# A weight sum of the down-projection taken from the in-projection's fourth block into its second, and the down-projection's buffers in two pools

## The chip, the cores and the metric

One Trainium2 chip, of which one core is used. The metric is the device time of one execution in microseconds (us). Everything is fp32; matmul operands are split into a high and a low fp32r part and multiplied as three matmuls.

## The reference, cut to what matters

One layer of a streaming encoder over 2048 prompt tokens and 8 x 16 sample tokens, width 1024:

```
z   = x @ w_in                      # 1024 -> 2824: mLSTM q, k, v, o, gates; attention q, k, v
mix = [mLSTM heads | sliding-window attention] @ w_out
h   = layer_norm(alpha * x + mix)
u   = h @ w_up                      # 1024 -> 5632, then a causal convolution of width 3
f   = (silu(gate) * value) @ w_down # 2816 -> 1024
y   = layer_norm(alpha * h + f)     # and the states of mLSTM, attention and convolution
```

## The kernel before, in words

The three large products are done with seven block products in the place of eight (a scheme of Strassen's kind), so they need sums and differences of quarters of the weights and of the tokens. The steps of one group carry the numbers 1 to 7 (variable `s`).

**In-projection** (`i_dense`). 17 tiles of 128 tokens stand in four blocks, b = 0 to 3, which the text calls first to fourth. A block has five groups of output columns (g = 0 to 4) and a group has seven products of 24 matmuls (`i_product`, L713). The weights are loaded into `wraw`, split by ScalarE (L218, high part) and VectorE (L219, low part) into a ring of eight halves `w`, four products' worth, and a half comes free when PE has done its product. Between the products, PE does the steps of three chains (mLSTM, attention, sample tokens) for tokens of the block before; ppt (L1354) is a transpose in the attention, pht (L1188) one in the mLSTM, pnum (L1223) its numerator. The chain of the mLSTM's norm runs DVE (statistics L1162, mr L1171), POOL (ms L1172), ACT (hn L1178), PE (pht).

A block's tokens are loaded into four buffers `xr1` to `xr4` (`x_load`, L541), each there once, in the last group of the block before by program order, and turned into operands until the block's own direct products (L739) are done.

**Weight sums** (`d_sums`). The down-projection needs 11 pairs of summed weight rows, kept in DRAM as `zt`. One sum loads two rows of 512 KB (`txy`, L854 and L855), makes four VectorE subtractions in place (L860 to L863) and stores both (L865, L866). While the in-projection runs, its two tiles are taken from the buffers `xr1` and `xr3`; its three parts stand behind the products 6, 5 and 3 of a group. Four of the 11 sums are done there, seven in the out-projection. A counter gives out the row pairs, so that the n-th sum takes pair n wherever it stands.

**Order of the work.** PE's instructions are issued in program order (`manual_schedule`). Those of the other engines and of SP, which issues nearly all DMAs, are put in order by the framework's scheduler, by readiness and program order; each engine and SP then work through their queues in that order. Two tiles with the same tag and bufs=1 take turns in program order.

**Up- and down-projection** (`f_ups`, `f_downs`). The up-projection has two pools on one stack: `f2sb` (operands hh/hl of the products 2, 5 and 3, the halves u0 and u1, ua, ub) and above it `f3sb` (cc, th, the operands of product 4, the convolution's states). Its last steps are the convolution (L1939, L1941), the gate (L1966 to L1968) and the store of cc (L1969, L1971). Both pools are closed then, and `dsb` is opened in their place, with r2, r3, r4 (loaded token operands, L2013, 16.9 KB a partition each; r1 is elsewhere) and six tiles yacc of 4 KB (L2151). The down-projection works through seven products a block (DORDER 1, 2, 4, 6, 5, 3, 7) in six units each; `d_tokens` splits a unit of r into fu, `d_weights` loads and splits weights into uw, and L2099 copies the banks of product 1 before product 2 adds to them.

Of the kernel before, what the change touches and what calls it, by code (L numbers as in the profile page):

```python
# [8 lines left out]
F32 = mybir.dt.float32  # L9
# [5 lines left out]
P = 128  # L15
D = 1024
# [189 lines left out]
class Prog:  # L206
# [20 lines left out]
    def run(self):  # L227
        PS = bass.MemoryType.PSUM
        nb = len(OBLOCKS)
        with ExitStack() as es:  # L230
            def enter(*a, **k):
                cm = self.pool(*a, **k)
                return cm.__enter__(), cm
            close = lambda cm: cm.__exit__(None, None, None)
            self.cp = es.enter_context(self.pool("const"))
            self.dp = es.enter_context(self.pool("dram", space=bass.MemoryType.DRAM))
            es.enter_context(self.tc.manual_schedule(engines={mybir.EngineType.PE}))
            self.setup()
            self.wp = es.enter_context(self.pool("wsb"))
            self.dps = es.enter_context(self.pool("dps", 3, PS))  # L240
            self.tp, tcm = enter("tsb", side="right")
            self.tps, tpcm = enter("tps", 5, PS)
            self.xp, xcm = enter("xsb")
            self.mp, mcm = enter("isb")
            chains = Chains(self)
            self.xs, self.gates, self.i_done = {}, {}, 0
            self.i_begin()
            self.warm_up()
            chains.weave(self.i_dense())
            close(mcm)  # L250
            wx, wxcm = enter("wx1sb")
            self.unit_more(wx)
            self.mp, mcm = enter("osb")
            self.o_setup()
            for b in range(nb - 1):
                chains.weave(self.late_done(self.o_block(b)))
            chains.until(NPT - 1)
            chains.drain()
            close(tpcm)
            close(tcm)  # L260
            self.fp, fcm = enter("fsb", side="right")
            self.fup, fpcm = enter("fup", 3, PS)
            self.f_setup()
            dense = self.o_block(nb - 1)
            first = self.f_hT(0)
            next(first)
            n = 0
            for i, _ in enumerate(dense):
                if i >= 2:
                    next(first, None)  # L270

                if i in (4, 7, 10):
                    self.f_tokens(0, *{4: (1,), 7: ("t1",), 10: ("t3", 7, "t2", 6)}[i])

                if i >= 22 and n < (2, 4, 5)[min((i - 22) // 4, 2)]:
                    self.f_next()
                    n += 1
            for _ in first:
                pass
            assert not self.norms  # L280
            close(mcm)
            close(wxcm)
            close(xcm)

            self.wx, wxcm = enter("wx2sb")
            self.f2, f2cm = enter("f2sb")
            self.f3, f3cm = enter("f3sb")
            self.f_ups(n)
            close(f3cm)
            close(f2cm)  # L290
            self.f2, f2cm = enter("dsb")
            self.f_downs()
            for cm in (f2cm, wxcm, fpcm, fcm):
                close(cm)


# [294 lines left out]
    def i_dense(self):  # L591
        nc, a = self.nc, self.a
        nb = len(IBLOCKS)
# [34 lines left out]
        for item in self.items:  # L628
            if after:

                after[0] -= 1
                if after[0] == 3:
                    self.logs_of(after[1] - 1)
                if after[0] < 0:
                    self.i_done = after[1]
                    after = None
            self.chains.hold = item[0] == "t" and item[1] > 0
            if item[0] == "t":
                _, b, ti, e = item
                if ("g", e, 3) not in self.wu:  # L640
                    self.advance()
                if b not in self.gates:
                    self.gates[b] = self.tp.tile([P, 5, 8], F32, name="gates", tag="gates", bufs=2)
                if b == 0 and ti == 1:
                    for h in range(2):
                        for i in range(2):
                            yield from self.i_direct(b, i, e, self.ib[i * 2], (h,))
                    self.i_keys(b, 0, self.ib[0])
                    self.i_keys(b, 1, self.ib[2])
                    self.advance()  # L650
                    continue
                ps = self.bank([P, 512], "pg") if ti == 4 else self.ib[ti % 2 * 2]
                yield from self.i_direct(b, ti, e, ps)
                self.i_keys(b, ti, ps)
                if ti == 3 and b or ti == 4:
                    self.release(4)
                    self.x_steps(b, 4)
                    if b:
                        self.x_steps(b, 5)
                self.advance()  # L660
                continue
            _, b, g, s = item
            if item not in self.wu:
                self.advance()
            yield from self.i_product(b, g, s)
            del self.wu[item]
            self.release(2)
            if self.trans and s != 4:
                self.i_transposes()
            with self.tc.high_priority():  # L670
                behind = self.i_after(b, g, s)
            if (b, g, s) == (0, 0, 7):
                self.t_setup()
            if (g, s) == (last, 4):
                after = [8, b + 1]
            if g == last and b + 1 < nb:
                if s == 7:
                    for i in (0, 2):
                        self.rope_load(IBLOCKS[b + 1][i], 2)
                for x in passages[b > 0].get(s, ()):  # L680
                    if x == "load":
                        self.spare = True
                        self.x_load(b + 1, 1, 2, 3, 4)
                    else:
                        self.x_steps(b + 1, x)
            if g == last and b + 1 == nb and s in (7, 5, 2, 3):
                self.x_pair(0, (7, 5, 2, 3).index(s))
            with self.tc.issue_after(behind) if behind and b == 0 else nullcontext():
                self.advance()

            if (b, g) in ((nb - 2, 1), (nb - 1, 0), (nb - 1, 1), (nb - 1, 2)):

                steps = (6, 5, 3)
                if s in steps:
                    self.d_sums(sums, steps.index(s))
                    sums += s == steps[2]
# [1305 lines left out]
    def d_load(self, b, q, u):  # L2002

        h, one = self.d_shape(b)
        if u == 0:
            pool, tag = (self.fp, "hraw") if q == 1 else (self.f2, f"r{q}")
            self.dr[b, q] = pool.tile([P, NK2, 384], F32, name=f"r{q}", tag=tag, bufs=1)
        r = self.dr[b, q]
        k0 = 0 if q in (1, 3) else NK2
        c0 = 0 if q in (1, 2) else h  # L2010
        ks = slice(DUNITS[u][0], DUNITS[u][-1] + 1)
        z = self.zf[b][k0:k0 + NK2][ks].rearrange("k p m -> p k m")
        self.nc.sync.dma_start(r[:, ks, :h], z[:, :, c0:c0 + h])  # L2013
        if one and q in (1, 2):
            self.nc.sync.dma_start(r[:, ks, h:h + one], z[:, :, 2 * h:])
# [46 lines left out]
            self.d_load(*l)  # L2062

    def f_downs(self):
        nc, a, f2 = self.nc, self.a, self.f2
        V, S = nc.vector, nc.scalar
        mm = nc.tensor.matmul
        ln2 = []
# [9 lines left out]
        nb, nu = len(FBLOCKS), len(DUNITS)  # L2078
        ys, ops = {}, {}
# [63 lines left out]
        for g, (b, s, u) in enumerate(self.dseq):  # L2143
# [3 lines left out]
            ts = [*tiles[:np_], *tiles[2 * np_:]] if s == 1 else tiles[np_:2 * np_] if s == 2 else []  # L2147
            if 0 <= u - 2 < len(ts):
                t = ts[u - 2]
                ys[t] = f2.tile([P, D], F32, name="yacc", tag="yacc", bufs=6)  # L2150
                nc.sync.dma_start(ys[t], self.zh[t])  # L2151
            if g == 3 * nu:
                for n in ("ln2_g", "ln2_b"):
                    t = self.fp.tile([P, D], F32, name="f_" + n, tag="hst", bufs=2)
# [53 lines left out]
```

## Time and profile before

| | before |
|---|---|
| median of 3 runs | 2300.78 us (2300.11 to 2303.31) |
| the profiled execution | 2301.44 us |
| its span, first to last instruction | 2299.7 us |
| TensorE busy | 2275.3 us (99%) |
| VectorE busy | 1810.8 us (79%) |
| ScalarE busy | 1272.3 us (55%) |
| GpSimd busy | 277.5 us (12%) |
| mean granted TensorE clock | 0.998 |
| DMA | 631.30 MB, 275 GB/s |

The span is the time between the first and the last instruction; the execution's own time is 1.7 us longer. PE is the matmuls on TensorE, PEld its weight loads, DVE is VectorE, ACT ScalarE, POOL GpSimd, SP SyncE. L713 is line 713 of the kernel. out<-in are the tiles that an instruction writes and reads. In the list of waits a row reads: who waited, for whom, us in total, times, the longest one. In the chain of waits a row is: start, us, what. In the timeline: start, us, instruction, and in brackets how long the engine stood idle before it and what ended that.

### The profile page before, as it was taken

How to read it: one execution, taken by the hardware profiler on the slowest of the kernel's cores; microseconds unless marked ns; L12 is line 12 of the kernel's file. 1: busy time of each engine (PE TensorE's matmuls, PEld its weight loads, DVE VectorE, ACT ScalarE, POOL GpSimd, SP SyncE). 2: the span in 40 equal slices, each digit the busy share in tenths (PEclk: the TensorE clock that was granted, in tenths of full speed). 3: DMA queues.
4: the chain of work that ended last, by engine and by line, in shares of the span. 5: the costliest groups of instructions: out<-in, count | busy, mean ns of one | idle time of the engine just before them, and what ended most of it. 6: DMA issues, size and time to landing. Idle time of an engine off the chain costs nothing.

```text
span 2299.7 us, 39828 instructions
## 1 busy us (share of the span) xinstructions
PE 2275.3 (99%) x14293; PEld 2090.5 (91%) x14293; DVE 1810.8 (79%) x3068; ACT 1272.3 (55%) x2373; POOL 277.5 (12%) x509
## 2 busy tenths in 40 slices
PE   8999999999999999999999999999999999999998
PEld 8999999989878778999999999999999978888876
DVE  8787677777688888998778777678766786895987
ACT  5453476766776656555656555556555544444442
POOL 0001001010121210211112000003211200200100
PEclk9999999999999999999999999999999999999999
DMA  7988998899998867898777999988998786757742
GB/s 283 318 304 289 302 327 276 276 309 305 324 324 266 279 212 279 300 331 300 280 273 269 305 300 310 311 267 288 320 295 262 248 298 212 251 173 222 256 153 86
DMA packets 302901, 631.30 MB, mean 275 GB/s; under 512 B 48172, under 2 KB 141424, under 8 KB 302704
## 3 DMA queue, kind: packets, MB, share of 16 engines
q1 hardware_dynamic: 298032, 615.06, 79.1%
q0 software_dynamic: 3520, 10.56, 1.5%
q10 hardware_dynamic: 1152, 3.15, 0.4%
q8 instruction: 113, 1.85, 0.3%
q14 instruction: 84, 0.69, 0.1%
HBM read 457.02 MB, written 171.64 MB: 273 GB/s over the span
## 4 chain that ended last, share of the span: by engine, by line
PE 84%; DVE 2%; DMA 2%; issue 0%; ACT 0%; POOL 0%; SPq 0%; DVEq 0%; POOLq 0%; ACTq 0%
PE dps L1883 20%; PE fup L1883 20%; PE dps L713 9%; PE dps L2091 7%; PE fup L2091 6%; PE fht L2091 6%; PE dps L223 3%; PE dps L225 2%; PE dps L224 2%; PE ppo L1360 1%; PE psc L1315 1%; PE ppt L1354 1%; PE dps L739 1%; PE fht L1707 1%; PE pscore L1140 1%; PE pnum L1223 1%
## 5 line engine op out<-in xcount | busy, mean ns | idle before, releaser
L1883 PE MATMUL fup<-hh,uw 128*128 128x384 f32 (+1 forms) x1848 | 478.2, 328 | 0.0
L1883 PE MATMUL dps<-hh,uw 128*128 128x384 f32 (+1 forms) x1848 | 478.0, 328 | 0.0
L1883 PEld LDWEIGHTS fup<-hh,uw 128*128 128x128 f32 x1848 | 330.3, 188 | 0.0
L1883 PEld LDWEIGHTS dps<-hh,uw 128*128 128x128 f32 x1848 | 330.1, 188 | 0.0
L1883 PE MATMUL fup<-hl,uw 128*128 128x384 f32 (+1 forms) x924 | 302.9, 328 | 0.9 <-DVE hl L219 0.9
L1883 PE MATMUL dps<-hl,uw 128*128 128x384 f32 (+1 forms) x924 | 302.8, 328 | 0.0
L1941 DVE SCALAR_TENSOR_TENSOR cc<-u,cw,cc 128x768 f32<-128x768 f32 (+1 forms) x264 | 258.1, 978 | 38.8 <-ACT cc L1939 30.5
L713 PE MATMUL dps<-w,oh 128*128 128x256 f32 x1344 | 254.7, 285 | 0.0
L218 ACT CAST uw<-wraw 128x1024 fp32r<-128x1024 f32 x126 | 123.2, 978 | 230.1 <-PE dps L2091 122.2
L219 DVE TENSOR_TENSOR w<-wraw,w 128x1024 fp32r<-128x1024 f32 (+2 forms) x163 | 186.3, 1150 | 65.7 <-ACT w L218 63.3
L218 ACT CAST w<-wraw 128x1024 fp32r<-128x1024 f32 (+2 forms) x163 | 160.2, 991 | 114.1 <-PE dps L713 53.6
L713 PEld LDWEIGHTS dps<-w,oh 128*128 128x128 f32 x1344 | 210.8, 188 | 11.0 <-issue 8.1
L219 DVE TENSOR_TENSOR uw<-wraw,uw 128x1024 fp32r<-128x1024 f32 x126 | 142.4, 1131 | 62.1 <-ACT uw L218 61.9
L713 PE MATMUL dps<-w,ol 128*128 128x256 f32 x672 | 188.2, 280 | 0.0
L1883 PEld LDWEIGHTS fup<-hl,uw 128*128 128x128 f32 x924 | 173.6, 188 | 1.7 <-DVE hl L219 1.6
L2091 PE MATMUL fup<-uw,fu 128*128 128x512 f32 x726 | 173.9, 396 | 1.3 <-ACT fht L2099 1.3
L1883 PEld LDWEIGHTS dps<-hl,uw 128*128 128x128 f32 x924 | 173.8, 188 | 0.0
L713 PE MATMUL dps<-oh,w 128*128 128x256 f32 x896 | 167.6, 283 | 2.9 <-DVE w L219 2.2
L2091 PEld LDWEIGHTS fup<-uw,fu 128*128 128x128 f32 x726 | 136.5, 188 | 34.3 <-ACT fht L2099 1.8
L2091 PE MATMUL dps<-uw,fu 128*128 128x512 f32 x660 | 164.9, 396 | 0.0
L2091 PEld LDWEIGHTS dps<-uw,fu 128*128 128x128 f32 x660 | 124.2, 188 | 29.7
L713 PEld LDWEIGHTS dps<-oh,w 128*128 128x128 f32 x896 | 140.0, 188 | 9.6 <-issue 4.9
(320 smaller groups left out, 4569.0 us busy)
## 6 DMA issues: line engine op xcount, KB each, us to landing
uw<-zw SPq DMA_DIRECT2D x176, 512.0 KB, 4.8
zw<-uw SPq DMA_DIRECT2D x88, 512.0 KB, 3.5
w<-zws SPq DMA_DIRECT2D x72, 512.0 KB, 6.0
wv<-wup SPq DMA_DIRECT2D x66, 512.0 KB, 5.0
wraw<-wi SPq DMA_DIRECT2D x65, 512.0 KB, 5.2
wraw<-zt SPq DMA_DIRECT2D x60, 512.0 KB, 3.8
wraw<-wdn SPq DMA_DIRECT2D x45, 512.0 KB, 4.5
wraw<-wo SPq DMA_DIRECT2D x40, 512.0 KB, 4.7
```

The lines of the kernel that those rows point to most:

```text
L218: nc.scalar.copy(hi, src)
L219: return nc.vector.tensor_sub(lo, src, hi.bitcast(F32)).ins
L223: mm(out, ah, bh, start=start, stop=False)
L224: mm(out, ah, bl, start=False, stop=False)
L225: mm(out, al, bh, start=False, stop=stop)
L713: mm(o, l, r, start=s in (1, 7) and c == k == i == 0, stop=k == 3 and i == 2, skip_group_check=True)
L739: mm(o, x, w, start=k == i == 0, stop=k == KD - 1 and i == 2, skip_group_check=True)
L1140: self.nc.tensor.matmul(ps[:, h], qk[:, 4 + h], qk[:, h], start=True, stop=True)
L1223: nc.tensor.matmul(ps[:, i], sd[:, h], v1[:, h], start=True, stop=t == 0)
L1883: mm(ps, l[:, k], r[:, k], start=s in (1, 7) and k == 0 and i == 0, stop=k == 3 and i == 2, skip_group_check=True)
L1941: V.scalar_tensor_tensor(c[:, v], u[:, i:i + n], w[i], c[:, v], op0=ALU.mult, op1=ALU.add)
L2091: mm(ps, l[:, k, c], r[:, k], start=s in (1, 4, 7) and u == 0 and k == 0 and i == 0, stop=u == nu - 1 and k == n - 1 and i == 2, skip_grou ...
```

## The change

In `i_dense` the four places of the in-projection's sums were (block, group) = (2, 1), (3, 0), (3, 1), (3, 2) with b counted from 0; they are now (1, 1), (2, 1), (3, 0), (3, 2). In `run` the pool `dsb` gives way to two, `d2sb` and `d3sb`, opened one above the other; r2 and r3 are in the first, r4 and yacc in the second.

```diff
@@ run
             close(f3cm)
             close(f2cm)
-            self.f2, f2cm = enter("dsb")
+            self.f2, f2cm = enter("d2sb")
+            self.f3, f3cm = enter("d3sb")
             self.f_downs()
-            for cm in (f2cm, wxcm, fpcm, fcm):
+            for cm in (f3cm, f2cm, wxcm, fpcm, fcm):
                 close(cm)
@@ i_dense
-            if (b, g) in ((nb - 2, 1), (nb - 1, 0), (nb - 1, 1), (nb - 1, 2)):
+            if (b, g) in ((1, 1), (nb - 2, 1), (nb - 1, 0), (nb - 1, 2)):
 
                 steps = (6, 5, 3)
                 if s in steps:
                     self.d_sums(sums, steps.index(s))
@@ d_load
-            pool, tag = (self.fp, "hraw") if q == 1 else (self.f2, f"r{q}")
+            pool, tag = (self.fp, "hraw") if q == 1 else (self.f3 if q == 4 else self.f2, f"r{q}")
             self.dr[b, q] = pool.tile([P, NK2, 384], F32, name=f"r{q}", tag=tag, bufs=1)
@@ f_downs
-        nc, a, f2 = self.nc, self.a, self.f2
+        nc, a = self.nc, self.a
...
-                ys[t] = f2.tile([P, D], F32, name="yacc", tag="yacc", bufs=6)
+                ys[t] = self.f3.tile([P, D], F32, name="yacc", tag="yacc", bufs=6)
```

## The prediction

> **What bounds the kernel now.** I read the page first, then the stretches of 50 us, the list of what TensorE waited for, and the chain of waits around the two places that the diff touches.
>
> ```profile
> span 2299.7 us, 39828 instructions
> PE 2275.3 (99%) x14293; PEld 2090.5 (91%) x14293; DVE 1810.8 (79%) x3068; ACT 1272.3 (55%) x2373; POOL 277.5 (12%) x509
> 500.00:550.00 50.00, 46.50 (x378) 42.06 (x379) 31.54 (x104) 31.55 (x81) 5.43 (x9) 0.97 0.94 320
> 1850.00:1900.00 50.00, 48.69 (x209) 39.01 (x208) 47.48 (x55) 24.90 (x32) 0.00 (x0) 1.00 0.78 287
> PE ppt L1354 <- ACT pth L1355: 2.7, 1, 2.7
> PE pht L1188 <- ACT hn L1178: 1.3, 3, 0.5
> PE pnum L1223 <- issue: 1.0, 1, 1.0
> PE ppt L1354 <- DVE C L1235: 0.8, 1, 0.8
> PE fup L2091 <- ACT fht L2099: 1.3, 1, 1.3
> ```
>
> In the stretches the columns after the length are the busy times of PE, PEld, DVE, ACT and POOL, then the granted clock, the DMA share and GB/s. TensorE is busy 2275.3 of 2299.7 us and its instructions are not touched, nor is their order, which is written out by hand. So the change can move only idle PE time, and 24.4 us is all there is. The two windows hold 3.5 and 1.3 us of it. The waits name it: 2.7 + 0.8 us in front of two attention transposes in the fourth in-projection block (b=3), 1.3 us at the start of the down-projection. The 1.0 and the 1.3 us (pnum, pht) belong to the third block (b=2).
>
> The idle time near 512 us has a sequel. These are stretches of 2 us, with PE alone, clock, DMA share, GB/s:
>
> ```profile
> 512.00:514.00 2.00, 0.00 (x0) 1.00 1.05 385
> 514.00:516.00 2.00, 1.82 (x6) 0.57 0.92 291
> 516.00:518.00 2.00, 2.00 (x9) 0.57 0.55 217
> 518.00:520.00 2.00, 2.00 (x19) 1.00 0.77 242
> ```
>
> Behind the 2.7 us without a matmul the granted clock is 0.57 for 4 us: 4 x 0.43 = 1.7 us of work lost that no list of waits shows. The stall at that place therefore costs 2.7 + 0.8 + 1.7 = 5.2 us.
>
> Who caused it stands in the chain of waits (start, us, what):
>
> ```profile
> 474.75 7.13 DMA zt<-txy
> ...
> 481.94 5.79 DMA txy<-wdn
> ...
> 493.44 4.89 DMA zt<-txy
> ...
> 498.34 5.49 DMA txy<-wdn
> ...
> 503.93 0.69 DVE txy L860
> ...
> 509.85 2.50 POOL ms L1172
> ...
> 513.66 0.48 ACT pth L1355
> ...
> 514.18 1.06 PE ppt L1354 x4
> ```
>
> txy are the two rows of the down-projection's weight sum, in the buffers xr1 and xr3, one of each. In the fourth block three sums run through that one pair: load, four DVE subtractions, store, next load. The third sum's load leaves at 498.34, as the second's store has landed, and DVE stands in front of its first subtraction:
>
> ```profile
> 503.93 0.69 DVE L860 TENSOR_TENSOR txy<-txy 128x512 f32<-128x512 f32 x1 [3.79 <-DMA txy<-wdn]
> ```
>
> Behind it in DVE's queue are the statistics, the state update C (whose lateness is the 0.8 us) and the scale mr, on which POOL's ms, ACT's hn and pth and then PE's ppt wait in a line.
>
> **The change, part by part.** *(a) The fourth block loses one of its three sums.* Two loads of 512 KB, four DVE operations and two stores go. The sums that remain are the first and the one of group 2. The trace shows that a sum's load is issued as soon as its buffers are free and not at its place in the program: 481.94 follows the store at once (474.75 + 7.13 = 481.88). So I expect the group 2 sum where the middle one ran, 482 to 498 us, and nothing of the kind after that. That frees DVE of 3.79 us of waiting and 4 x 0.69 = 2.8 us of work ahead of the stalled transposes, 6.6 us in all, of which 3.79 + 0.69 stand ahead of C and mr. POOL's ms may shorten too: it took 2.50 us beside the last three subtractions, and elsewhere in the chain
>
> ```profile
> 330.82 1.06 POOL ms L1172
> ```
>
> A lead of 4.5 us and more against idle times of 0.8 and 2.7 us: both go, and with them the slow clock. After that the list of PE's waits, which I asked for up to 560 us, names nothing that would be late next. Value: -5.2 us (bounds -5.2 and 0).
>
> On the clock the Trainium skill ("TensorE: Matmul & The Clock Gate", Part 1) says that the array falls to half rate after an idle window of about 3.4 us, a window that runs freely. By its letter a gap of 2.7 us need not have done it, and (a) would be worth 3.5 us. The trace has the 0.57 right behind this gap, though the 0.8 us lie not far before it; the 1.3 us of idle time in the stretch at 1850 left the clock at 1.00.
>
> *(b) The second block gains a sum*, at group 1. Its loads take the buffers xr1 and xr3 when the block's own tokens are through with them. The nearest rows:
>
> ```profile
> 167.12 0.42 SPq L541 DMA_DIRECT2D xr<-xq  x1
> ...
> 174.67 1.05 ACT L218 CAST w<-wraw 128x1024 fp32r<-128x1024 f32 x1 [1.67 <-PE dps L713]
> ...
> 175.76 1.23 DVE L219 TENSOR_TENSOR w<-wraw,w 128x1024 fp32r<-128x1024 f32 x1 [0.33 <-ACT w L218]
> 252.67 2.83 PE dps L713 x24
> DMA to landing us min/median/max: 5.0/6.1/7.6
> 312.37 0.69 DVE L860 TENSOR_TENSOR txy<-txy 128x512 f32<-128x512 f32 x1 [2.76 <-DMA txy<-wdn]
> 166.00:301.00 135.00, 134.16 (x1214) 128.22 (x1213) 96.05 (x184) 62.61 (x116) 15.30 (x14) 1.00 0.90 302
> 463.00:620.00 157.00, 153.50 (x1274) 140.61 (x1273) 110.07 (x317) 108.49 (x274) 16.14 (x28) 0.99 0.94 314
> ```
>
> At 167.12 the third block's tokens are already being loaded, some 70 us ahead of their place. In the new program the sum stands ahead of them in the same two buffers, so its loads go out there (about 167 to 172) and those two token loads behind the sum's stores, some 15 to 20 us later; they are used only in the block's last group, so that hides. On SP the weight loads stand behind whatever waits there for a store to land; on DVE everything stands behind L860. A sum's load takes 6.1 us to land (the row of L854), so DVE may stop as it does in the third block, 2.76 us, and works 2.8 us more: at most 5.6 us if it all fell into one place. What bears on PE first is the weights' split. Its room: the split starts when PE releases the buffer (1.67 us idle, ended by PE), takes 1.05 on ACT and 1.23 on DVE, and three products of 24 matmuls, 3 x 2.83 = 8.5 us, run meanwhile. 8.5 - 2.3 = 6.2 us of room against 5.6. So the weights should just hold, if the subtractions come in pieces as they did elsewhere. The other reading is the third block's sum, after whose wait PE lost 1.0 us (pnum). There ACT and DVE carry the attention's work too; in the second block ACT is busy 63 of 135 us, DVE 96. Price between 0 and the 5.9 us of rival 4 below, with the third sum's 5.2 in the fourth block as the nearest dear row; below nothing it can't be, since that block loses no work. I take +0.5, between none and the third block's 1.0. The 2 MB that it moves are 2 / 0.30 = 6.6 us of DMA at the window's 302 GB/s, in 135 us at a share of 0.90: room for it, not much.
>
> *(c) Two pools in the down-projection.* The old pool dsb lies over both pools of the up-projection, f2sb and f3sb. The first loads of r2 (L2013) stood for the last user of the two, the store of the last cc, a tile of f3sb:
>
> ```profile
> SPq L2013 <- DMA zf<-cc: 3.8, 1, 3.8
> ...
> 1842.33 4.33 SPq L2013 DMA_DIRECT2D r<-zf  x8
> 1832.60 0.90 DVE L1941 SCALAR_TENSOR_TENSOR cc<-u,cw,cc 128x656 f32<-128x656 f32 x1
> ...
> 1845.78 0.83 ACT L218 CAST fu<-r 128x768 fp32r<-128x768 f32 x1 [4.59 <-DMA r<-zf]
> ...
> 1850.34 1.04 ACT L218 CAST uw<-wraw 128x1024 fp32r<-128x1024 f32 x1
> 1851.28 1.06 ACT L2099 COPY fht<-fup 128x512 f32<-128x512 f32 x2
> ```
>
> By the shapes f2sb has 47.6 KB a partition and r2 with r3 33.8 KB, so d2sb fits into f2sb's room alone, and f2sb's last reader is the convolution at 1832.60 + 0.90 = 1833.5 us at the latest. r2's loads can leave nearly 9 us before 1842.3. ACT, idle for 4.59 us before its casts of r2 and then crowded, gets them over earlier, and the copy L2099, which stood behind the weights' cast of 1850.34 and for which PE waited 1.3 us, runs when its bank is done. yacc and r4 still wait for cc's store, in d3sb; they stand behind r2 on SP now as they did before. Value between -1.3 and 0; I take -1.0, since the copy alone may still hold PE for a part.
>
> **Sum**: -5.2 + 0.5 - 1.0 = -5.7 us. The profiled execution took 2301.44 us, 1.7 more than its span, and 0.7 more than the median, 2300.78. From the median: 2295.1 us. Below 0.2%, 4.6 us, a measurement of this kernel tells nothing from no change; -5.7 is only just past that.
>
> **The rivals.**
>
> 1. *The wait moves instead of going*: the sum of group 2 slides to where the third one ran, or its first subtraction stands in front of another transpose. For it: DVE stopped for a sum's load in two different blocks, 2.76 and 3.79 us, so the order on DVE was made for faster loads. Against it: the two sums now have the buffers of three. Then (a) is worth nothing: 0.5 - 1.0 = -0.5, 2300.3 us.
>
> 2. *The slow clock had another cause* than this gap and stays: -3.5 + 0.5 - 1.0 = -4.0, 2296.8 us. For it: only that one gap is there to tell by. Against it: the slow 4 us begin where the gap ends. The window of the Trainium skill ("TensorE: Matmul & The Clock Gate", Part 1) would have it so.
>
> 3. *The two pools change nothing*, because r2's loads wait for all that was freed before them, or stand behind cc's store on SP: -5.2 + 0.5 = -4.7, 2296.1 us. For it: SP issues in order and cc's stores are ahead in the program.
>
> 4. *Slower*: in the second block DVE is stopped for the whole landing. If L860 comes to the head of DVE's queue as soon as its load is issued, DVE stands up to 7.6 us and works 2.8: 10.4 us against 6.2 us of room, 4.2 us of idle PE, and the slow clock after that, 1.7: +5.9. It decides from 6.2 us of DVE time in one place. With the fourth block's stall kept as in rival 1 and (c) as reckoned: 5.9 - 1.0 = +4.9, 2305.7 us. For it: DMA there is at 0.90 before any sum. Against it: the longest stop in the trace is 3.79 us.
>
> **How the numbers follow.** Forecast 0.50, rival 1 0.20, rival 2 0.05, rival 3 0.08, rival 4 and other slips of the same sort 0.17. The forecast's own range is 2292 to 2298: the 2.3 idle microseconds of the third block may go or double, as the schedule shifts. Faster by over 0.2%: 0.45 of the forecast's 0.50 and half of rival 3, 0.49. Slower by over 0.2%: rival 4, 0.17. The rest, 0.34, is within. For 8 in 10 the range goes from 2292.0 (all three terms at their best, -6.5, and the third block's 2.3 us gone) to 2304, between rival 1 and rival 4.
>
> **What would show it.** (a): no PE wait on pth near 510 us, clock 1.00 through the fourth block, one chain of two sums there, and no third load near 498. (b): a load of txy near 167 to 172 us, a DVE stop below 4 us, PE busy over 134 of the block's 135 us. (c): L2013 first issued before 1842 by some microseconds, less wait of PE on L2099. The forecast is wrong if PE loses more than 2 us in the second block, or if the transposes of the fourth still wait for ACT.

## The result and the profile after

| | before | after |
|---|---|---|
| median of 12 runs | 2301.07 us (2300.11 to 2303.31) | 2295.70 us (2293.95 to 2300.79) |
| ratio | | 0.9975, interval 0.9968 to 0.9983 |
| the profiled execution | 2301.44 us | 2295.38 us |
| its span | 2299.7 us | 2293.6 us |

The changed kernel is faster by 5.4 us, a quarter of a per cent. The forecast was 2295.1 us. The interval reaches over the bound of 0.2% that the prediction set itself: the gain is sure, that it is more than 0.2% is likely only. In the changed kernel the lines of the code are one higher (L860 is now L861, and so on).

The page's first part, and the stretches that were shown of before (length; busy time of PE, PEld, DVE, ACT and POOL; granted clock, DMA share, GB/s):

```profile
span 2293.6 us, 39821 instructions
PE 2273.8 (99%) x14293; PEld 2090.5 (91%) x14293; DVE 1809.7 (79%) x3068; ACT 1272.2 (55%) x2373; POOL 274.1 (12%) x509
...
166.00:301.00 135.00, 134.16 (x1214) 128.24 (x1213) 98.16 (x188) 62.61 (x116) 15.30 (x14) 1.00 0.92 318
500.00:550.00 50.00, 50.00 (x416) 45.39 (x416) 33.63 (x109) 35.27 (x93) 4.41 (x10) 1.00 0.93 310
1850.00:1900.00 50.00, 50.00 (x216) 40.34 (x215) 48.15 (x58) 21.58 (x26) 0.00 (x0) 1.00 0.72 253
```

The number of matmuls is the same. The stretch at 500 us was busy for 46.50 us at a clock of 0.97 and is now full at 1.00; that at 1850 went from 48.69 to 50.00. The second block's stretch, which took in the new sum, has the same 134.16 us of PE as before: in that block the sum costs PE nothing.

What PE waited for (us in total, times, the longest), first from 150 to 560 us, then from 560 us to the end:

```profile
PE pht L1189 <- ACT hn L1179: 1.3, 3, 0.5
PE ppt L1528 <- POOL scs L1522: 0.8, 1, 0.8
PE pnum L1224 <- issue: 0.6, 1, 0.6
...
PE fup L1884 <- DVE hl L219: 0.9, 2, 0.6
PE ppt L1355 <- ACT sc L1333: 0.7, 1, 0.7
PE fup L1884 <- ACT ub L1913: 0.6, 1, 0.6
```

The waits on pth and on C in the fourth block are gone, and so is the one on fht (L2099 before). Two small ones came up: ppt on sc grew from 0.3 to 0.7 us, and the one on ub is new.

Where the time came from is seen best by the same matmul in both traces, its start after less its start before: -0.2 us at 497 us, -6.0 at 518, -5.5 at 677, -4.6 ahead of the down-projection's start, -6.1 behind it (1852 us) and at the end. So the fourth block gave 5.8 us, small waits near 677 and 1617 us took 0.5 and 0.9 back, and the down-projection's start gave 1.5.

The chain of waits of the changed kernel around the old stall (start, us, what) now holds PE alone:

```profile
499.92 4.77 PE dps L714 x42
504.69 0.87 PE ppt L1355 x8
...
506.11 3.42 PE dps L714 x30
509.53 0.87 PE ppt L1355 x8
```

In its timeline stand the stops of DVE at the subtractions of the sums, in the second, third and fourth block, and POOL's ms:

```profile
172.50 0.69 DVE L861 TENSOR_TENSOR txy<-txy 128x512 f32<-128x512 f32 x1 [0.64 <-DMA txy<-wdn]
178.79 0.69 DVE L862 TENSOR_TENSOR txy<-txy 128x512 f32<-128x512 f32 x1 [1.01 <-DMA txy<-wdn]
311.84 0.69 DVE L861 TENSOR_TENSOR txy<-txy 128x512 f32<-128x512 f32 x1 [2.23 <-DMA txy<-wdn]
487.58 0.69 DVE L861 TENSOR_TENSOR txy<-txy 128x512 f32<-128x512 f32 x1 [1.87 <-DMA txy<-wdn]
506.40 1.04 POOL L1173 TENSOR_TENSOR ms<-mr,mhalf 128x4 f32<-128x4 f32 x1 [6.31 <-DVE mr L1172]
```

The fourth block's one remaining stop of this kind is 1.87 us, 16 us earlier than the old one of 3.79 us was. The kernel before has it too: DVE stopped for 1.74 us at 487.75 us, ahead of its middle sum, and PE waited for nothing there. And ms takes 1.04 us where it took 2.50.

At the start of the down-projection, in the timelines of SP and ACT:

```profile
1826.11 0.45 SPq L1972 DMA_DIRECT2D zf<-cc  x1
1826.73 3.18 SPq L2014 DMA_DIRECT2D r<-zf  x5
1834.13 0.33 SPq L1970 DMA_DIRECT2D zf<-cc  x1
...
1843.92 1.05 ACT L218 CAST uw<-wraw 128x1024 fp32r<-128x1024 f32 x1 [2.42 <-PE fup L2092]
1844.88 1.06 ACT L2100 COPY fht<-fup 128x512 f32<-128x512 f32 x2
```

r2's first loads now leave between two stores of cc, at 1826.7 us; before, it was 1842.3 us, after the last of them. With 4.6 us of the difference taken off, which the kernel was ahead by then, that is some 11 us earlier. The copy for which PE had waited starts 6.4 us earlier than before, 1.8 us of it won here.

### The profile page after: what moved, and what is told of

It reads as the page before. It is cut to its first block, busy times and chain, and to the rows that moved or that the text cites. A ratio compares the mean times of both kernels' runs of the same rounds, so it can differ in the third digit from the quotient of the medians.

```text
span 2293.6 us, 39821 instructions
## 1 busy us (share of the span) xinstructions
PE 2273.8 (99%) x14293; PEld 2090.5 (91%) x14293; DVE 1809.7 (79%) x3068; ACT 1272.2 (55%) x2373; POOL 274.1 (12%) x509
## 4 chain that ended last, share of the span: by engine, by line
PE 85%; DVE 2%; DMA 1%; issue 1%; ACT 0%; POOL 0%; SPq 0%; DVEq 0%; POOLq 0%; ACTq 0%
PE dps L1884 20%; PE fup L1884 20%; PE dps L714 9%; PE fup L2092 7%; PE dps L2092 7%; PE fht L2092 6%; PE dps L223 3%; PE dps L225 2%; PE dps L224 2%; PE ppo L1361 1%; PE ppt L1355 1%; PE psc L1316 1%; PE dps L740 1%; PE fht L1708 1%; PE pnum L1224 1%
```

## The experiments

Three questions: whether the two parts give what they were reckoned at, by what mechanism the fourth block's third sum stalled PE (the buffers' turn, DVE's place in line, or the sheer work), and whether the slow clock belongs to the gap. Ratios are to the kernel before on the same chip.

### The sums alone (e1_sums)

```diff
-            if (b, g) in ((nb - 2, 1), (nb - 1, 0), (nb - 1, 1), (nb - 1, 2)):
+            if (b, g) in ((1, 1), (nb - 2, 1), (nb - 1, 0), (nb - 1, 2)):
```

> The kernel before with only the sums moved; the one pool of the down-projection stays. Theory (the third sum of the fourth block stood DVE up on its load, and that stall with the slow clock behind it was most of the difference): the fourth block's PE waits on ACT pth and DVE C are gone and the clock is 1.00 there, about -4.7 us, 2296.4; L2013 still waits some 3.8 us for cc's store and PE 1.3 us on L2099. Rival (the pools made the difference, the sums only trade places): 0, 2301.1, with a new PE wait in the second block.

Measured: 2297.71 us, ratio 0.9984, interval 0.9975 to 0.9993. By the same matmul, this kernel gains 5.7 us between 497 and 518 us (the changed kernel 5.8): the fourth block's term is whole without the pools. It lost some of it later. These are PE's waits behind 560 us and SP's on the last store of cc:

```profile
PE pnum L1223 <- DVE asm L1330: 1.5, 1, 1.5
PE fup L2091 <- ACT fht L2099: 1.0, 1, 1.0
...
SPq L2013 <- DMA zf<-cc: 3.4, 1, 3.4
```

The down-projection's wait stands as before, 1.0 us here, and a wait of 1.5 us at the start of the out-projection (633 us) is new. That one isn't in the changed kernel, whose sums run at the same places; I have no cause for it.

### The pools alone (e2_pools)

```diff
-            self.f2, f2cm = enter("dsb")
+            self.f2, f2cm = enter("d2sb")
+            self.f3, f3cm = enter("d3sb")
...
-            pool, tag = (self.fp, "hraw") if q == 1 else (self.f2, f"r{q}")
+            pool, tag = (self.fp, "hraw") if q == 1 else (self.f3 if q == 4 else self.f2, f"r{q}")
...
-                ys[t] = f2.tile([P, D], F32, name="yacc", tag="yacc", bufs=6)
+                ys[t] = self.f3.tile([P, D], F32, name="yacc", tag="yacc", bufs=6)
```

> The kernel before with only the two pools; the sums stay where they were. Theory: r2's loads leave some 11 us earlier, PE's 1.3 us on L2099 goes, the fourth block keeps its 3.5 us of waits and its slow clock: -1.0 to -1.3 us, 2299.9. Rival (loads behind cc's store on SP, nothing gained): 0. Rival (the pools made the whole difference): -5.4.

Measured: 2301.31 us, ratio 1.0001, interval 0.9992 to 1.0010: no gain in the total. In its trace PE's wait on L2100 is gone, and by the same matmul this kernel stands 2.2 us late just ahead of the down-projection's start and 0.7 us behind it: 1.5 us won on the spot. Most of the 2.2 us, 1.4, had been lost far away, near 335 us, at a place that the edit doesn't touch. Its stretches there:

```profile
334.00:336.00 2.00, 2.00 (x13) 0.79 1.02 305
336.00:338.00 2.00, 2.00 (x10) 0.50 0.95 297
```

(PE alone, clock, DMA share, GB/s.) That is a slow clock in the third block, which the trace of before doesn't have. The local gain is shown; whether it arrives in the total, a measurement with an interval of 4 us can't tell.

### yacc in the lower pool (e5_yacc)

The changed kernel, with yacc in d2sb, so that the lower pool no longer fits into the room of f2sb.

```diff
-                ys[t] = self.f3.tile([P, D], F32, name="yacc", tag="yacc", bufs=6)
+                ys[t] = self.f2.tile([P, D], F32, name="yacc", tag="yacc", bufs=6)
```

> The changed kernel with yacc in the lower of the two pools, d2sb, beside r2 and r3 (33.8 + 24.6 = 58.4 KB a partition, more than the 47.6 of f2sb under it). Theory (a pool waits for every pool that lies under it): r2's first load waits for cc's store again, near 1836 to 1838 us, PE loses about 1 us on L2099, the sums' gain stays: +1.0 to +1.3 us against the changed kernel, about 2297. Rival (having two pools is what counts, or it is worth nothing): 0, with r2's loads as early as in the changed kernel.

Measured: 2297.91 us, ratio 0.9980 (0.9971 to 0.9989), its interval over the changed kernel's. SP's wait and PE's are back:

```profile
SPq L2014 <- DMA zf<-cc: 3.6, 1, 3.6
...
PE fup L2092 <- ACT fht L2100: 0.7, 1, 0.7
```

r2's first loads leave at 1836.84 us, behind the last of cc's stores. So it isn't the number of pools that frees r2's loads, but that the lower one lies over f2sb alone.

By the same matmul against before, every run whose lower pool lies over f2sb alone gains 1.5 to 1.6 us at the down-projection's start (the changed kernel, e2, e6, e9, e10, e11), this one 0.6. The runs with the one old pool (e1, e3, e4, e8) gain 0.1 to 0.6 there, for the old wait itself varies: it is 0.7 to 1.2 us in these four and 1.3 in the trace of before. Against them the pools are worth 0.9 to 1.4 us.

### The middle sum in other buffers (e3_pair)

The kernel before, its three sums left in the fourth block; the middle one gets xr2 and xr4, so that the third doesn't wait for the middle one's store.

```diff
-... for p, tag, n in (pool(1), pool(3))]
+... for p, tag, n in ((pool(2), pool(4)) if k == 2 else (pool(1), pool(3)))]
```

> The kernel before, with the middle one of the fourth block's three sums in the buffers xr2 and xr4, the other two in xr1 and xr3 as before. All three sums stay in the fourth block, with the same DVE work and DMA traffic; only the third one's load need not wait for the second one's store. Theory (the wait for the buffers, and DVE in front of the load, made the stall): no DVE wait of 3.8 us near 500 us, PE's waits on pth and C gone or under 1 us, clock 1.00, -4 to -5 us, about 2296.5. Rival (2.8 us of DVE work and 2 MB too much in that block, wherever they stand): the stall stays, 0 to -1.5 us.

Measured: 2299.65 us, ratio 0.9995 (0.9986 to 1.0003). I had expected 4 to 5 us; the ratio gives 1.2, which is not to be told from nothing. The trace gains 3.4 us in the fourth block, having lost 1.5 to a slow clock near 335 us in the third. The third sum's loads did leave earlier (491.3 and 494.5 us, not 498.3 and 505.9), and the slow clock at 513 us is gone. But PE's waits and the timeline show:

```profile
PE ppt L1354 <- ACT pth L1355: 1.4, 1, 1.4
PE ppo L1360 <- ACT pth L1355: 0.3, 1, 0.3
...
494.49 8.04 DMA txy<-wdn
...
497.30 0.69 DVE L860 TENSOR_TENSOR txy<-txy 128x512 f32<-128x512 f32 x1 [1.30 <-DMA txy<-wdn]
502.62 0.69 DVE L861 TENSOR_TENSOR txy<-txy 128x512 f32<-128x512 f32 x1 [2.88 <-DMA txy<-wdn]
```

The second load took 8.04 us to land, and DVE stood twice, 1.30 + 2.88 = 4.2 us, with the state update and the scale behind it. POOL's ms took 2.50 us here as before, beside two of the subtractions; what part of the 1.4 us comes from that, this run can't tell. My reading is that the buffers' turn only made the load late, and that PE stalls because DVE comes to the subtraction before its load has landed. The next experiments put this mended theory to the test.

### The third sum one group later (e4_late)

```diff
-            if (b, g) in ((nb - 2, 1), (nb - 1, 0), (nb - 1, 1), (nb - 1, 2)):
+            if (b, g) in ((nb - 2, 1), (nb - 1, 0), (nb - 1, 1), (nb - 1, 3)):
```

> The kernel before, with the third sum of the fourth block put in group 3 in place of group 2. Theory (a sum's load leaves when its buffers come free, not at its place in the program): the third load still leaves within a few us of 498, DVE stands for it as before, PE loses 2 us or more near 512 us: 0 us against before, 2300 to 2302. Rival (the place in the program spaces the sums out): the third load some 30 us later, no stall at 512 us, -4 to -5 us.

Measured: 2301.32 us, ratio 0.9999 (0.9990 to 1.0008). The load left at 498.28 us as in the kernel before, and the stall stayed: PE's waits, the stop on DVE, the third sum's second subtraction, POOL's ms, and the stretches behind the stop.

```profile
PE ppt L1354 <- ACT pth L1355: 2.1, 1, 2.1
PE ppt L1354 <- DVE C L1235: 0.9, 1, 0.9
...
503.31 0.69 DVE L860 TENSOR_TENSOR txy<-txy 128x512 f32<-128x512 f32 x1 [3.87 <-DMA txy<-wdn]
...
516.17 0.69 DVE L861 TENSOR_TENSOR txy<-txy 128x512 f32<-128x512 f32 x1
...
509.24 1.90 POOL L1172 TENSOR_TENSOR ms<-mr,mhalf 128x4 f32<-128x4 f32 x1 [9.66 <-DVE mr L1171]
...
512.00:514.00 2.00, 1.04 (x4) 0.72 (x4) 0.09 (x1) 2.00 (x7) 0.19 (x1) 0.74 0.97 338
514.00:516.00 2.00, 2.00 (x6) 0.39 (x5) 1.77 (x3) 2.00 (x6) 0.19 (x1) 0.50 0.74 291
```

The group in the program moved neither the first load nor the first subtraction: the load went as soon as the buffers were free, and the subtraction stood in DVE's line as before. The other three subtractions did move, from 510.8 us to 516.2 and later, behind the stall.

### The third sum's subtractions behind a later addition (e8_later)

The kernel before, all three sums in place, same loads, stores and work; the third one's four subtractions come behind the addition of the same group's product 5 in DVE's queue.

```diff
             if g < 2:
-                V.scalar_tensor_tensor(u, C, KSCALE, u, op0=ALU.mult, op1=ALU.add)
+                self.added = V.scalar_tensor_tensor(u, C, KSCALE, u, op0=ALU.mult, op1=ALU.add).ins
             else:
-                V.tensor_add(u, C, u)
+                self.added = V.tensor_add(u, C, u).ins
...
+            with self.tc.issue_after(self.added) if k == 3 else nullcontext():
                 V.tensor_sub(x[:, l], x[:, r], x[:, l])
```

> The kernel before with all three sums in the fourth block in the same buffers; only the third one's four subtractions are put behind a later DVE operation, the addition (L784 or L786) of the same group's step 5, some 30 us later. Its loads and stores, the traffic and the DVE work stay. Theory, mended after e3_pair (what counts is that DVE stands in front of a load that has not landed, whoever delayed the load): no DVE stop of 3.8 us near 500 us, PE's waits on C and pth gone or under 0.5 us, clock 1.00 there, -4.5 to -5.2 us, 2296.5. Rival (a third sum is too much for that block, in traffic or DVE work, and e3_pair's remaining 1.4 us were that): a stall of 1 us or more, 2299 or above.

Measured: 2297.56 us, ratio 0.9978 (0.9969 to 0.9987), 5.1 us by the ratio and as much as the whole change. All that PE waited for between 150 and 560 us, and the stretches at the old stall:

```profile
PE pht L1188 <- ACT hn L1178: 1.3, 3, 0.5
PE pnum L1223 <- issue: 0.9, 1, 0.9
PE ppt L1527 <- POOL scs L1521: 0.8, 1, 0.8
...
512.00:514.00 2.00, 2.00 (x14) 1.03 (x12) 1.71 (x3) 2.00 (x5) 0.38 (x2) 1.00 0.93 354
514.00:516.00 2.00, 2.00 (x19) 1.86 (x17) 1.54 (x2) 2.00 (x7) 0.00 (x0) 1.00 1.04 395
```

In DVE's timeline, the first of the third sum's subtractions, with no idle time in brackets:

```profile
548.92 0.68 DVE L860 TENSOR_TENSOR txy<-txy 128x512 f32<-128x512 f32 x1
```

The subtractions run at 549 us without a stop. By the same matmul this kernel gains 5.8 us between 497 and 518 us, just as the changed kernel does, with all three sums, their traffic and the buffers' turn kept. So it is neither the number of sums nor their traffic, but what DVE has ahead of the stalled chain.

e8 takes the stop and the 2.8 us of work away from there together. e4 tells the two apart: there three of the four subtractions already ran behind the stall, and it gained 0.5 us of the 5.8 (ms took 1.90 us where it took 2.50). What still stood ahead of the statistics in e4 is one subtraction of 0.69 us and the stop of 3.87 us in front of it. That stop is the cause of nearly all of the stall; the work has a share of some 0.5 us. And the slow clock went with the gap, once more with all three sums in place.

### No sum in the second block (e6_nosum)

The changed kernel without the second block's sum; the down-projection reads a neighbouring pair in its place.

```diff
-                    self.d_sums(sums, steps.index(s))
+                    if b > 1:
+                        self.d_sums(sums, steps.index(s))
...
+        k0 += m is not None and u == 0
```

> The changed kernel without the sum in the second block. It leaves that pair's loads, subtractions and stores out, and the down-projection reads a neighbouring pair in its place, with as many loads as before. Theory (the new place costs nothing, the split's room hides it): as the changed kernel, 2295.7, within 0.5 us, and PE busy 134.2 of the second block's 135 us in both. Rival (the forecast's +0.5 or more is paid there): 0.5 to 2 us faster than the changed kernel.

Measured: 2295.23 us, ratio 0.9971 (0.9960 to 0.9983), against 0.9975 with the sum: the intervals overlap. The second block:

```profile
166.00:301.00 135.00, 134.16 (x1214) 128.20 (x1213) 96.05 (x184) 62.61 (x117) 15.30 (x14) 1.00 0.89 302
```

PE's 134.16 us are those with the sum. In its new block the sum costs nothing. Whether it costs something further on, the totals can't tell: this trace lacks the small waits near 677 and 1617 us, but other runs with the sum lack one of them too (e11 the first, e9 the second).

### Two better versions (e9_alllater, e10_later3, e11_after)

If DVE's stop for a load is the cause, the same remedy should take the third block's waits from the changed kernel. In e9 all four sums' subtractions go behind the later addition (the same diff with `if not ring`), in e10 only those of the third and fourth block (`if k and not ring`); e11 is the changed kernel once more, on e10's chip.

> The changed kernel with the subtractions of all four sums of the in-projection put behind the same addition of their group, so that DVE stands for no load there. Theory: no DVE stop for txy before 600 us; PE's wait before pnum near 318 us (0.6 us) goes, the pht waits near 333 us stay or shrink: 0 to -2 us against the changed kernel, 2294.7. Rival (the order on DVE that this upsets costs more): +1 or worse.

> The changed kernel with the subtractions of the sums in the third and fourth blocks put behind the addition of their group, as in e9_alllater, and the second block's left as in the changed kernel. Theory: the third block's PE waits on pnum and pht (0.6 to 1.0 and 1.3 us) mostly go, as they did in e9_alllater, where the second block lost as much again (0.7 us more before a transpose, 1.1 us before a product): -1.2 to -2.5 us against the changed kernel, about 2294. Rival (what e9_alllater won there came of its second block running late): 0.

> The changed kernel again, beside e10_later3 on the same chip: 0.9975 of the kernel before, the fourth block without a PE wait over 0.3 us, and a slow clock near 335 us in some executions, not in others.

Measured: e9 2295.70 us, ratio 0.9973 (0.9963 to 0.9984); e10 2292.51, ratio 0.9964 (0.9950 to 0.9977); e11 2296.97, ratio 0.9978 (0.9970 to 0.9987). PE's waits from 150 to 560 us in e9, then in e10:

```profile
PE ppt L1528 <- POOL scs L1522: 1.6, 1, 1.6
PE dps L714 <- DMA w<-zws: 1.1, 1, 1.1
PE pht L1189 <- ACT hn L1179: 0.4, 1, 0.4
```

```profile
PE ppt L1528 <- POOL scs L1522: 0.8, 1, 0.8
PE pht L1189 <- ACT hn L1179: 0.4, 1, 0.4
```

In both the third block's waits are nearly gone (pnum 0, pht 0.4 us of 1.3). e9 pays for it in the second block, with 0.8 us more on scs and a new wait of 1.1 us on a load of w, and ends level with the changed kernel; I have not followed by what path the later subtractions bring these waits. e10 leaves that block alone. On one chip e10 is 4.5 us ahead of the changed kernel by the medians, more than the 1.2 to 2.5 expected, and four of its five runs (2291.47 to 2292.65) lie below the lowest of e11's eleven (2294.09). The fifth, 2297.39 us, is the one that was profiled: it lost what it had gained in one wait of 2.9 us at 671 us (ppt on sc) and a slow spell of the clock twice as long as the others (6.83 us). So e10 beats both kernels in most runs; the intervals of the ratios overlap, and why the wait at 671 us came in that execution stays open.

## Why the prediction was right, point by point

*(a) Right in size, half right in cause.* -5.2 us was forecast, and the stretch gave 5.8 in the changed kernel and 5.7 with the sums alone. The two sums ran where they were expected, with no third load near 498 us. Of the two causes that stood side by side in the text, three sums in one pair of buffers and DVE standing in front of a load, the second is the cause (e8: all three sums kept, stall gone; e4: the stop kept, stall kept), and the first only one way to make the load late (e3: other buffers, part of the gain). The lead of 4.5 us and more was made in two places and not one: ms, which waits for mr, began 3.3 us earlier (506.40 in place of 509.85 us, less the 0.2 that the kernel was ahead), and it took 1.5 us less.

*(b) Mis-sized, on the safe side.* +0.5 us was forecast between 0 and 5.9. The sum's loads left where they were expected (167.1 and 171.9 us). Its stops of DVE were 0.64 and 1.01 us and not 2.76, the subtractions came in two pieces 6 us apart, and PE is busy for 134.16 us with and without the sum. That it was the room of 6.2 us that took them agrees with this, but no run varies the room. What was not in the sum are small waits that differ from trace to trace: 0.5 us at 672 us and 0.9 near 1612 (most of it on ub) in the changed kernel, 1.5 at 633 in e1 alone.

*(c) Right on the spot.* -1.0 us was forecast, and the down-projection's start gave 1.5 us in the changed kernel and with the pools alone, a little past the bound of 1.3. The way was the one forecast (r2's loads ahead of cc's last store; with yacc in the lower pool the wait is back, e5). That the total of the pools alone shows none of it (1.0001, interval 0.9992 to 1.0010) doesn't speak against the trace, but the total doesn't confirm it either.

*The rivals.* The wait did not move (rival 1): no PE wait on pth or C is left, and the stop that remained is of 1.87 us at 487 us, and PE waits for nothing behind it. It could have stayed: in e4 the sum's new place in the program left the stop and the stall where they were, and that kernel gained nothing. The slow clock had no other cause at that place (rival 2): it went with the gap in the changed kernel, in e1 and in e8, and came with it in e4. The Trainium skill ("TensorE: Matmul & The Clock Gate", Part 1) would have asked for an idle window of about 3.4 us; here gaps of 2.7 us (before) and 2.1 us (e4) had the slow clock behind them, and the measurement decides. r2's first loads did not stand behind the last of cc's stores (rival 3). DVE never stood for the whole landing in the second block (rival 4).

The sum of the trace is then -0.2 (ahead of 497 us) - 5.8 + 1.4 - 1.5 = -6.1, as by the spans; the medians differ by 5.4. That the total came so near to the forecast of -5.7 is in part luck: (a) and (c) gave 1.1 us more than forecast and (b) cost 0.5 less, and 1.4 us of small waits that the sum did not hold took most of it back.

## What to carry to other kernels

In these kernels an operation that nobody was waiting for stood in DVE's queue ahead of the landing of its load (3.79 us), and held up all that stood behind it: look in the timeline for idle time that ends on a DMA, and see who stands behind. Placing the consumer behind something later was worth as much as taking the work away (e8), and giving the load other buffers or another place in the program was not (e3, e4). The pool opened over two closed ones waited for the last user of both (SP's waits of 3.8 us in before and 3.6 in e5): put what is needed first into a pool that covers only what comes free first.

## What the clock showed

In these traces idle time well short of 3.41 us was enough for a slow clock. Apart from the end of each execution, the slow spells in the traces of before, e2, e3, e4, e8, e10 and e11 last 3.41 us (or twice that) at 0.5 and begin at whole multiples of 3.413 us from the first clock record: the one of before at the 149th, 508.59 us after that record, those near 335 us at the 96th. PE's idle time in the 3.413 us ahead of a spell was 2.66 us in before, 2.09 in e4 and 1.98 in e10. Near 335 us in the third block 1.33 to 1.44 us sufficed (e2, e3, e8, e11): the three waits on hn, 1.3 to 1.5 us together, fall into one such stretch there, or into two. These are rows of the stretch from 318 to 340 us in the changed kernel, profiled twice (the second row is e11):

```profile
318.00:340.00 22.00, 20.36 (x163) 18.28 (x164) 14.93 (x46) 16.69 (x45) 1.43 (x4) 1.00 0.98 333
```

```profile
318.00:340.00 22.00, 19.83 (x143) 17.89 (x144) 14.98 (x44) 16.15 (x44) 1.43 (x4) 0.92 0.94 330
```

The same kernel with the same waits on hn, once at 1.00 and once at 0.92, which is 22 x 0.08 = 1.8 us. In the first the fullest of these stretches of 3.41 us holds 0.93 us of idle time, in the second 1.33; so where the stretches fall may be part of the spread between runs of one kernel. The rule isn't settled: 1.46 to 1.58 us of idle time in one such stretch left the clock alone in e1, e5 and e9.
